# Seven block products in place of eight for the first layer's gate and up projections

## The chip, the cores and the metric

The kernel runs on one core of one Trainium2 chip. Its metric is the device time of one execution in microseconds (us); the comparison goes by the median of several runs. The engines are named as in the profile: PE (TensorE, matmul) with PEld (its weight loads), DVE (VectorE), ACT (ScalarE), POOL (GpSimd) and SP (SyncE, which issues the DMAs). Each engine takes its instructions in a fixed order.

## The reference

A backbone of two layers over 512 latent tokens and 256 context tokens, width 1024. Each layer has a mixing sub-layer and a SwiGLU sub-layer of inner width 2816. The context goes through the whole first layer; the second layer puts out the latent tokens alone.

```
def swiglu(h, w_gate, w_up, w_down):
    return (jax.nn.silu(h @ w_gate) * (h @ w_up)) @ w_down

x = x + g1 * (jnp.concatenate([y_a, y_b, y_c], axis=-1) @ w_out)
x = x + g2 * swiglu(modulate(x, norm2_g, sh2, sc2), w_gate, w_up, w_down)
...                          # the same for the context xc, while ctx_out
# modulate(x, g, shift, scale) = rms_norm(x, g) * (1 + scale) + shift
# mod = silu(c) @ w_mod[l] + b_mod[l]: shift, scale and gate of both sub-layers
```

## The kernel before

Features lie on the 128 partitions and tokens on the free axis, so `x` is eight tiles (k = 0 to 7) of 128 x 768. Every large product is done in fp32 accuracy by three matmuls of a shorter type: `split` writes a high half by an ACT copy and a low half by a DVE subtract, and hi·hi, hi·lo and lo·hi are summed in PSUM. `wload` loads a weight block of 128 x 1024 from DRAM (SP) into one of the `wraw` buffers and splits it (ACT L128, DVE L129). `dense` (L152) takes a block over nk steps of k, for each the three matmuls, for each 512 latent and then 256 context columns.

A SwiGLU sub-layer has 22 column blocks of gate and of up. In the first layer the blocks are worked through in three pieces, `FF_PIECES` = (0,8), (8,8), (16,6). Within a piece each block does gate, up, then `silu` on ACT, the product with up on DVE (L1177) and a split of the result into `gh`, `gl` (L108, L109). The first three blocks run as a wave (L402): all three advance with each k, while `norm2` delivers the normed k from DVE. At the end of a piece eight `dense` calls form the piece's share of the down projection, and `resid` adds each to `x` in SBUF (L1100).

The next layer's modulation rows (`mod_steps`) are computed beside this on DVE: a step loads a 512 KB block of `w_mod` and does one or two products with the sum over the free axis (L212, output to `junk` or in place). The steps wait in a list `fill`; each `dense` pops one (`FILL_FF` = 1). `lagged` runs w_out and the last piece of the down projection: it does the latent part of the last k before the context part, so that the norm that follows can begin.

The order of an engine's instructions comes from a list scheduler over the program, with its own costs; buffers come from pools, and SP issues all DMAs in one order, so a transfer that waits holds up those behind it.

Of the kernel before, what the change touches and what calls it, by code (L numbers as in the profile page):

```python
# [9 lines left out]
F32 = mybir.dt.float32  # L10
# [7 lines left out]
D = 1024  # L18
# [25 lines left out]
def tile_backbone(ctx: ExitStack, tc: tile.TileContext, A, out):  # L44
# [10 lines left out]
    wk = ctx.enter_context(tc.tile_pool(name="wk", bufs=7))  # L55
    tok = ctx.enter_context(tc.tile_pool(name="tok", bufs=1))
# [44 lines left out]
    def zct(name, dt=F32):  # L101
        return zc.tile([128, ZU], dt, tag="z", name=name)
# [97 lines left out]
    c_all = const.tile([128, 2, D], F32, name="c_all")  # L200
    junk = const.tile([128, D], F32, name="junk")

    def mod_steps(l, vs):
# [3 lines left out]
        def step(v, i):  # L207
# [3 lines left out]
            for t in range(nt):  # L211
                ve.scalar_tensor_tensor(  # L212
                    out=junk if t < nt - 1 else raw, in0=raw, scalar=1.0, in1=c_all[:, t, :], op0=ALU.mult, op1=ALU.mult,
                    accum_out=modT[:, v * 8 + i, t:t + 1])
# [228 lines left out]
    for l in range(2):  # L443
# [215 lines left out]
        def do_Crows():  # L659
            i64 = zct("i64")[:, 0:384].rearrange("p (c s) -> p c s", c=6)  # L660
            f64 = zct("f64")[:, 0:384].rearrange("p (c s) -> p c s", c=6)
            gp.memset(i64, 0.0)
# [434 lines left out]
        def resid(pss, k, row, gs):  # L1097
            for ps, g in zip(pss, gs):
                xs = xsl(k, g)
                ve.scalar_tensor_tensor(  # L1100
                    out=xs, in0=ps, scalar=modT[:, row * 8 + k, g[3]:g[3] + 1], in1=xs, op0=ALU.mult, op1=ALU.add)
# [39 lines left out]
        steps2 = []  # L1141
        preload(AF.Sqrt, tabled)
        lagged(lambda k: wload(A["w_out"][l, k]), KD,
               lambda g: (lambda k: yv(g, k, 0), lambda k: yv(g, k, 1), g[2]), 2, norm2, *TRAIL[2 * l])
        h_next = {}
        hp2 = [hpart(h2, g) for g in groups]
        W_g, W_u = A["w_gate"][l], A["w_up"][l]
        fill_rate[0] = FILL_FF
        if not last:
            fill.extend(mod_steps(0, (5,)) + mod_steps(1, range(6)))  # L1150
        for pi, (f0, nf) in enumerate(FF_PIECES):
# [97 lines left out]
def layout(inputs):  # L1249
# [18 lines left out]
    def ksplit(w, nk):  # L1268
# [34 lines left out]
```

## Time and profile before

| | before |
|---|---|
| median of 3 runs | 1716.52 us |
| lowest, highest | 1714.64, 1721.14 us |
| profiled execution | 1715.26 us |
| its span, granted clock | 1713.5 us, 0.988 |
| PE busy | 1654.2 us (97%), 10784 matmuls |
| DVE busy | 940.7 us (55%), 1697 instructions |
| DMA | 184.11 MB, mean 107 GB/s |

The span is what the profiler saw between the first and the last instruction; the execution's own time is a little longer. Busy shares are means over stages with different limits: the first layer's SwiGLU sub-layer runs from about 449 us to 1012 us, the second layer's ends the program. A timeline row gives start, duration, engine, line, operation and tiles, and in brackets the idle time ahead of it and what ended that. Durations of rows that follow each other overlap a little, so the difference of two starts is the pace.

### The profile page before, as it was taken

How to read it: one execution, taken by the hardware profiler on the slowest of the kernel's cores; microseconds unless marked ns; L12 is line 12 of the kernel's file. 1: busy time of each engine (PE TensorE's matmuls, PEld its weight loads, DVE VectorE, ACT ScalarE, POOL GpSimd, SP SyncE). 2: the span in 40 equal slices, each digit the busy share in tenths (PEclk: the TensorE clock that was granted, in tenths of full speed). 3: DMA queues.
4: the chain of work that ended last, by engine and by line, in shares of the span. 5: the costliest groups of instructions: out<-in, count | busy, mean ns of one | idle time of the engine just before them, and what ended most of it. 6: DMA issues, size and time to landing. Idle time of an engine off the chain costs nothing.

```text
span 1713.5 us, 26246 instructions
## 1 busy us (share of the span) xinstructions
PE 1654.2 (97%) x10784; PEld 1413.0 (82%) x10784; DVE 940.7 (55%) x1697; ACT 609.2 (36%) x1123; POOL 154.9 (9%) x157
## 2 busy tenths in 40 slices
PE   7998999999999999999999999989989999999998
PEld 5886777778888888888888889767869988888888
DVE  4599788654665654434443365765585633333335
ACT  5455344643432211221122344534554522222235
POOL 0001112133100000000000120013043000000000
PEclk9999999999999999999999999989999999999999
DMA  8741323122153334333332234111113322222222
GB/s 301 247 157 56 119 82 104 49 84 75 65 160 123 123 127 134 125 129 126 123 123 90 75 108 125 61 50 46 62 62 124 107 97 99 98 99 93 92 83 96
DMA packets 57143, 184.11 MB, mean 107 GB/s; under 512 B 6720, under 2 KB 8384, under 8 KB 56896
## 3 DMA queue, kind: packets, MB, share of 16 engines
q1 hardware_dynamic: 57024, 182.45, 32.5%
q8 instruction: 84, 1.38, 0.3%
q14 instruction: 35, 0.29, 0.0%
HBM read 175.08 MB, written 7.34 MB: 106 GB/s over the span
## 4 chain that ended last, share of the span: by engine, by line
PE 79%; DVE 10%; issue 3%; ACT 3%; DMA 2%; POOL 1%; SPq 0%; DVEq 0%; ACTq 0%; POOLq 0%
PE dps L152 63%; PE wps L402 5%; PE vps L647 3%; DMA wmod<-in_w_mod 1%; DVE wlo L129 1%; PE bops L542 1%; PE ptps L584 1%; PE bsps L542 1%; DVE nm L569 1%; PE nps L896 1%; DVE junk L212 1%; DVE rM L715 1%; DVE rF L706 1%; ACT pu L882 1%; ACT prob L572 1%
## 5 line engine op out<-in xcount | busy, mean ns | idle before, releaser
L128 ACT ACTIVATE whi<-wraw 128x1024 fp32r<-128x1024 f32 (+2 forms) x224 | 226.6, 1013 | 716.1 <-PE dps L152 450.1
L129 DVE TENSOR_TENSOR wlo<-wraw,whi 128x1024 fp32r<-128x1024 f32 (+2 forms) x224 | 264.8, 1183 | 164.1 <-ACT whi L128 160.6
L152 PE MATMUL dps<-h2ll,whi 128*128 128x512 f32 (+1 forms) x664 | 259.4, 392 | 0.0
L152 PE MATMUL dps<-h2lh,wlo 128*128 128x512 f32 (+1 forms) x664 | 258.9, 392 | 0.0
L152 PE MATMUL dps<-h2lh,whi 128*128 128x512 f32 (+1 forms) x664 | 257.9, 390 | 0.0
L152 PE MATMUL dps<-gh,wlo 128*128 128x512 f32 (+1 forms) x576 | 175.2, 340 | 0.0
L152 PE MATMUL dps<-gl,whi 128*128 128x512 f32 (+1 forms) x576 | 175.0, 340 | 0.0
L152 PE MATMUL dps<-gh,whi 128*128 128x512 f32 (+1 forms) x576 | 174.7, 340 | 0.0
L212 DVE SCALAR_TENSOR_TENSOR wmod<-wmod,c_all 128x1024 f32<-128x1024 f32 x80 | 98.9, 1236 | 101.1 <-DMA wmod<-in_w_mod 100.3
L152 PEld LDWEIGHTS dps<-h2lh,wlo 128*128 128x128 f32 x664 | 124.3, 188 | 28.4
L152 PEld LDWEIGHTS dps<-h2lh,whi 128*128 128x128 f32 x664 | 124.3, 188 | 28.2
L152 PEld LDWEIGHTS dps<-h2ll,whi 128*128 128x128 f32 x664 | 124.3, 188 | 26.9
L1100 DVE SCALAR_TENSOR_TENSOR x<-dps,modT,x 128x512 f32<-128x512 f32 (+1 forms) x112 | 65.3, 596 | 137.8 <-PE dps L152 137.5
L152 PE MATMUL dps<-lh,whi 128*128 128x512 f32 x336 | 136.8, 408 | 0.3 <-DVE ck L783 0.3
L152 PE MATMUL dps<-ll,whi 128*128 128x512 f32 x336 | 135.5, 403 | 1.2 <-DVE ll L109 1.2
L152 PE MATMUL dps<-lh,wlo 128*128 128x512 f32 x336 | 134.5, 400 | 0.0
L152 PEld LDWEIGHTS dps<-gl,whi 128*128 128x128 f32 x576 | 99.3, 188 | 13.3 <-DVE gl L109 0.2
L152 PEld LDWEIGHTS dps<-gh,wlo 128*128 128x128 f32 x576 | 99.3, 188 | 13.1
L152 PEld LDWEIGHTS dps<-gh,whi 128*128 128x128 f32 x576 | 99.1, 188 | 13.2
L212 DVE SCALAR_TENSOR_TENSOR junk<-wmod,c_all 128x1024 f32<-128x1024 f32 x48 | 58.8, 1225 | 78.4 <-DMA wmod<-in_w_mod 78.3
L1177 DVE TENSOR_TENSOR silu<-silu,dps 128x512 f32<-128x512 f32 (+1 forms) x64 | 37.3, 588 | 107.7 <-PE dps L152 107.7
L152 PE MATMUL dps<-h2cl,whi 128*128 128x256 f32 x328 | 92.8, 283 | 0.0
(320 smaller groups left out, 3108.7 us busy)
## 6 DMA issues: line engine op xcount, KB each, us to landing
wmod<-in_w_mod SPq DMA_DIRECT2D x80, 512.0 KB, 3.6
wraw<-in_w_up SPq DMA_DIRECT2D x42, 512.0 KB, 3.2
wraw<-in_w_gate SPq DMA_DIRECT2D x40, 512.0 KB, 3.2
wraw<-in_win_blk SPq DMA_DIRECT2D x34, 512.0 KB, 3.7
wraw<-in_w_down SPq DMA_DIRECT2D x32, 512.0 KB, 3.2
wraw<-in_w_out SPq DMA_DIRECT2D x19, 512.0 KB, 3.3
wraw<-in_w_down SPq DMA_DIRECT2D x21, 384.0 KB, 3.0
wraw<-in_win_cv SPq DMA_DIRECT2D x16, 408.0 KB, 3.2
```

The costliest lines, as they stand in the source:

```text
L128: ac.activation(out=hi[:, 0:n], in_=raw[:, 0:n], func=AF.Copy)
L129: ve.tensor_tensor(out=lo[:, 0:n], in0=raw[:, 0:n], in1=hi[:, 0:n].bitcast(F32), op=ALU.subtract)
L152: m = te.matmul(out=ps[:, 0:T], lhsT=wt[:, c], rhs=(flo if wh else fhi)(k), start=(k == 0 and wi == 0), stop=(k == nk - 1 and wi == 2),)
L212: ve.scalar_tensor_tensor(out=junk if t < nt - 1 else raw, in0=raw, scalar=1.0, in1=c_all[:, t, :], op0=ALU.mult, op1=ALU.mult, accum_out= ...
L402: m = te.matmul(out=ps[:, 0:T], lhsT=wt[:, cs_], rhs=(flo if wh else fhi)(k), start=(k == 0 and wi == 0), stop=(k == KD - 1 and wi == 2))
L542: m = te.matmul(*args, **kw)
L569: ve.tensor_reduce(out=nm, in_=sps[:, 0:n], axis=AX.X, op=ALU.max, negate=True)
L572: ac.activation(out=pt[:, 0:n], in_=sps[:, 0:n], func=AF.Exp, bias=nm, accum_out=sm_)
L584: te.transpose(out=tps[:, i * 128:(i + 1) * 128], in_=pt[:, i * 128:(i + 1) * 128], identity=ident)
L647: te.matmul(out=vps[i][:, 0:408], lhsT=tokslice(nm, k, i), rhs=wt[:, cs], start=(k == 0 and wi == 0), stop=(k == KD - 1 and wi == 2))
L1100: ve.scalar_tensor_tensor(out=xs, in0=ps, scalar=modT[:, row * 8 + k, g[3]:g[3] + 1], in1=xs, op0=ALU.mult, op1=ALU.add)
L1177: ve.tensor_tensor(out=s, in0=s, in1=pui, op=ALU.mult)
```

## The change

Only the first layer's SwiGLU sub-layer is rebuilt (`ffn_seven`), and what has to make room for it.

- Two column blocks are a pair and the tokens two halves of 384. The eight k are four even-odd couples j. So gate (or up) of a pair is a 2 x 2 by 2 x 2 block product, done with seven products P1 to P7 instead of eight. A `Unit` is the gate or the up of one pair, 22 in all. Each product is 4 j x 3 matmuls of 384 columns (L1260).
- The weight operands are sums of blocks: `s1`, `s2`, and a difference written over half of the second block (DVE L1239 to L1241), then `s4` (L1251); all are split. The activation operands T1 to T4 (L1185 to L1190) are made once, after the norm, by `operands`; B11, B21 and B22 are plain halves.
- The seven results meet in three PSUM tiles X, Y, Z. `snap` copies a partial sum out (ACT), `put` adds the other part (DVE L1285), multiplies with gate (L1289) and splits.
- `pin` fixes the order of the products on PE: P6 P5 P7 of a unit, P1 P2 of the next unit, then P4 P3 of the first.
- Six pieces of 2, 4, 4, 4, 4 and 4 column blocks (`FF0_PIECES`). `x` no longer stays in SBUF: for each k of a piece's down stage it is loaded from DRAM into `xs` (L1426), gets the residual (L1106) and is stored (L1428); the last piece loads it into tiles again.
- The pools: `wraw` 3 to 4 buffers, from which `junk` is now taken too; `wk` 7 to 9; small tiles moved into others.
- The eight steps of modulation row 5 of layer 0 move from the SwiGLU sub-layer to the mixing sub-layer, ahead of w_out. Layer 1's 48 steps stay in `fill`.

```
 FF_PIECES = [(0, 8), (8, 8), (16, 6)]
+FF0_PIECES = [(0, 2)] + [(f, 4) for f in range(2, 22, 4)]
+HN = 384
...
-    wraw = ctx.enter_context(tc.tile_pool(name="wraw", bufs=3))
+    wraw = ctx.enter_context(tc.tile_pool(name="wraw", bufs=4))
...
+        def operands(j):
+            e, o = hf[2 * j], hf[2 * j + 1]
+            n1, n2 = slice(0, HN), slice(HN, 2 * HN)
...
+                if ops[0] == "T1":
+                    ve.tensor_tensor(out=t[:, n1], in0=e[:, n2], in1=e[:, n1], op=ALU.subtract)
+                    ve.tensor_tensor(out=t[:, n2], in0=o[:, n2], in1=t[:, n1], op=ALU.subtract)
...
+                split(hi, lo, t[:, 0:2 * HN])
...
+            def sums(self):
+                a, b = self.a, self.b
+                self.s1, self.s2 = wkt("s1"), wkt("s2")
+                ve.tensor_tensor(out=self.s1, in0=b[:, 0:512], in1=b[:, 512:1024], op=ALU.add)
+                ve.tensor_tensor(out=self.s2, in0=self.s1, in1=a[:, 0:512], op=ALU.subtract)
+                ve.tensor_tensor(out=b[:, 0:512], in0=a[:, 0:512], in1=b[:, 0:512], op=ALU.subtract)
...
+            def put(self, q, d, ps):
+                g = self.spot(q)
+                if d is not None:
+                    ve.tensor_tensor(out=d if self.up else g, in0=d, in1=ps[:, 0:HN], op=ALU.add)
+                if not self.up:
+                    ac.activation(out=g, in_=ps[:, 0:HN] if d is None else g, func=AF.Silu)
+                    return
+                ve.tensor_tensor(out=g, in0=g, in1=ps[:, 0:HN] if d is None else d, op=ALU.mult)
+                th, tl = [t[q // 2][:, (q % 2) * HN:(q % 2) * HN + HN] for t in tiles(self.pr)]
+                split(th, tl, g)
...
+                        u.stage2()      # P6, P5, P7
+                        feed(1)
...
+                            nxt.stage1()    # P1, P2 of the next unit
+                        u.stage3()      # P4, P3
+                        if nxt is not None and i < nf - 1:
+                            nxt.fin1()
...
+                    for k in range(KD):
+                        xt = zat("xs")
+                        sp.dma_start(out=xt, in_=xd[k])
+                        resid(dense(dload(k), nf, [gpart(g) for g in whole], mm if k % 2 == 0 else mx), k, 5, whole, xt)
+                        sp.dma_start(out=xd[k], in_=xt)
...
+        if not last:
+            fill.extend(mod_steps(0, (5,)))
...
-            fill.extend(mod_steps(0, (5,)) + mod_steps(1, range(6)))
+            fill.extend(mod_steps(1, range(6)))
```

How this stands on DVE is shown at three places. A row has the line, the operation, output and inputs with buffer numbers, the shape, and the waits: PE and Activation are engines, DMAHW a DMA. The first place is the opening, just behind the second norm of the first layer. Before, the context part of the norm is written (`hn`, then its low half `h2cl` or `h2ll`):

```order
L286 SCALAR_TENSOR_TENSOR hn_4715<-x0_4136,a2_231,rb_4697 128x256 [waits Activation_49]
L286 SCALAR_TENSOR_TENSOR hn_4741<-x1_4137,a2_231,rb_4697 128x256
L286 SCALAR_TENSOR_TENSOR hn_4827<-x4_4140,a2_231,rb_4620 128x512
L288 SCALAR_TENSOR_TENSOR h2cl_4687<-hn_4715,modT_227,h2ch_4686 128x256 [waits Activation_49]
L288 SCALAR_TENSOR_TENSOR h2cl_4687<-hn_4741,modT_227,h2ch_4686 128x256 [waits Activation_49]
L286 SCALAR_TENSOR_TENSOR hn_4773<-x2_4138,a2_231,rb_4697 128x256 [waits DVE_49]
```

After, behind all of the norm (`hf`), the operands follow (T1 and T2 in one tile `t`, T3 and T4 in the next):

```order
L1185 TENSOR_TENSOR t_4934<-hf_4671 128x384
L1189 TENSOR_TENSOR t_4939<-hf_4672,hf_4671 128x384
L1186 TENSOR_TENSOR t_4934<-hf_4672,t_4934 128x384 [waits DVE_49]
L114 TENSOR_TENSOR ocl_4791<-hf_4678,och_4790 128x384
L1190 TENSOR_TENSOR t_4939<-hf_4672,t_4934 128x384 [waits DVE_49]
L114 TENSOR_TENSOR wlo_5053<-wraw_4804,whi_5052 128x1024 [waits Activation_49]
L114 TENSOR_TENSOR oll_4670<-t_4934,olh_4669 128x768 [waits Activation_49]
L114 TENSOR_TENSOR ol_4943<-t_4939,oh_4942 128x768 [waits Activation_49]
```

Sums of operands and two low halves of 768 now stand between the norm and the products P6 and P5 of a j; the list repeats for each j.

The second place is the down stage of the first piece. Before, for each k (24 matmul pairs of `dps` on PE) one low half, one step of modulation and one residual:

```order
L129 TENSOR_TENSOR wlo_6122<-wraw_6119,whi_6121 128x1024 [waits DMAHW4_49,Activation_49]
L212 SCALAR_TENSOR_TENSOR junk_104,modT_228<-wmod_6299,c_all_103 128x1024 [waits DMAHW1_49]
L212 SCALAR_TENSOR_TENSOR wmod_6299,modT_228<-wmod_6299,c_all_103 128x1024 [waits DVE_49]
L1100 SCALAR_TENSOR_TENSOR x3_4139<-dps_6001,modT_227,x3_4139 128x512 [waits PE_49]
L1100 SCALAR_TENSOR_TENSOR x3_4139<-dps_6002,modT_227,x3_4139 128x256 [waits PE_49]
L129 TENSOR_TENSOR wlo_6184<-wraw_6181,whi_6183 128x1024 [waits DMAHW6_49,Activation_49]
```

After, with 12 matmuls for a k, and one low half (512 wide) for two k:

```order
L1106 SCALAR_TENSOR_TENSOR xs_5279<-dps_5282,modT_226,xs_5279 128x256 [waits PE_49]
L216 SCALAR_TENSOR_TENSOR junk_5297,modT_227<-wmod_5295,c_all_103 128x1024 [waits DMAHW6_49,DVE_49]
L216 SCALAR_TENSOR_TENSOR wmod_5295,modT_227<-wmod_5295,c_all_103 128x1024 [waits DVE_49]
L134 TENSOR_TENSOR wlo_5308<-wraw_5305,whi_5307 128x512 [waits DMAHW2_49,Activation_49]
L216 SCALAR_TENSOR_TENSOR junk_5327,modT_227<-wmod_5325,c_all_103 128x1024 [waits DMAHW3_49,DVE_49]
L216 SCALAR_TENSOR_TENSOR wmod_5325,modT_227<-wmod_5325,c_all_103 128x1024 [waits DVE_49]
L1106 SCALAR_TENSOR_TENSOR xs_5303<-dps_5311,modT_226,xs_5303 128x512 [waits DMAHW4_49,DMAHW0_49,PE_49]
L1106 SCALAR_TENSOR_TENSOR xs_5303<-dps_5312,modT_226,xs_5303 128x256 [waits PE_49]
```

The low half for k = 4 and 5 (`wlo_5308`) stands behind the residual of k = 3, which waits for PE, and behind a modulation step; the residual now waits for a load of `xs` too.

The third place is within a pair, where gate hands over to up. Before, in a column block of the first piece (`silu` times up, low halves of weights and of `gl`):

```order
L1177 TENSOR_TENSOR silu_5142<-silu_5142,dps_5087 128x512 [waits PE_49,Activation_49]
L129 TENSOR_TENSOR wlo_5286<-wraw_5283,whi_5285 128x1024 [waits DMAHW2_49,PE_49,Activation_49]
L109 TENSOR_TENSOR gl_5141<-silu_5142,gh_5140 128x512 [waits Activation_49]
L1177 TENSOR_TENSOR silu_5147<-silu_5147,dps_5028 128x256
L212 SCALAR_TENSOR_TENSOR junk_104,modT_227<-wmod_5398,c_all_103 128x1024 [waits DMAHW5_49]
```

After, in the fifth piece, from the end of P2 of an up unit (`Y_8051`) to the low half that its P6 needs (`wlo_8125` from `s2_8120`); `Z_8006` is the gate unit's last product, P3:

```order
L1285 TENSOR_TENSOR sn_8064<-sn_8064,Y_8051 128x384 [waits PE_49,Activation_49]
L1289 TENSOR_TENSOR gate_7978<-gate_7978,sn_8064 128x384 [waits DVE_49]
L114 TENSOR_TENSOR gl_8115<-gate_7978,gh_8113 128x384 [waits Activation_49]
L1239 TENSOR_TENSOR s1_8119<-wraw_8043 128x512 [waits DMAHW0_49]
L1240 TENSOR_TENSOR s2_8120<-s1_8119,wraw_8042 128x512 [waits DVE_49]
L1241 TENSOR_TENSOR wraw_8043<-wraw_8042,wraw_8043 128x512
L114 TENSOR_TENSOR wlo_8125<-s1_8119,whi_8124 128x512 [waits Activation_49]
L1285 TENSOR_TENSOR gate_8004<-gate_8004,Z_8006 128x384 [waits PE_49]
L114 TENSOR_TENSOR wlo_8125<-s2_8120,whi_8124 128x512 [waits Activation_49]
```

Before, the low half of the next block's weights needs only its transfer, its high half and a free buffer; now the sums, a result that waits for P2 and one that waits for P3 stand ahead of it.

More of the change, by code (lines that the diff above doesn't have):

```diff
@@ L212, in step @@
                 ve.scalar_tensor_tensor(
-                    out=junk if t < nt - 1 else raw, in0=raw, scalar=1.0, in1=c_all[:, t, :], op0=ALU.mult, op1=ALU.mult,
+                    out=wraw.tile([128, D], F32, tag="w", name="junk") if t < nt - 1 else raw, in0=raw, scalar=1.0, in1=c_all[:, t, :], op0=ALU.mult, op1=ALU.mult,
                     accum_out=modT[:, v * 8 + i, t:t + 1])
@@ L1103, in tile_backbone, with lagged @@
         h2 = {}
-        def lagged(load, nk, part, row, done, tr, pos, eng=gp):
+        def lagged(load, nk, part, row, done, tr, pos, eng=gp, between=None):
             ga, gb = groups
@@ L1127, in lagged @@
                     done(ga, ssq[0])
+                if between is not None:
+                    between()
             done(gb, ssq[1])
@@ L1141, in tile_backbone, with norm2_seven, step @@
         steps2 = []
+        O, hf = {}, []
+        def norm2_seven(g, ssq):
+            s, o, T, m = g
+            n = 10 if m == 0 else 5
+            th = hyp.tile([128, n, HN], F32R, tag=s + "h", name="o" + s + "h")
+            tl = hyp.tile([128, n, HN], F32R, tag=s + "l", name="o" + s + "l")
+            O[s] = (th, tl)
+            if m == 0:
+                hf.extend(zct("hf") for _ in range(KD))
+            bc = ssq.finish(s)
+            def step(k):
+                v = hf[k][:, 512 * m:512 * m + T]
+                ve.scalar_tensor_tensor(
+                    out=v, in0=xsl(k, g), scalar=a2s[l][:, k, m:m + 1], in1=bc, op0=ALU.mult, op1=ALU.mult)
+                ac.activation(out=v, in_=v, func=AF.Identity, bias=modT[:, 3 * 8 + k, m:m + 1])
+                if m == 0:
+                    split(th[:, k, :], tl[:, k, :], hf[k][:, 0:HN])
+                    O["B%d1" % (1 + k % 2), k // 2] = (th[:, k, :], tl[:, k, :])
+                else:
+                    sp.dma_start(out=xd[k], in_=x[k][:, 0:768])
+            steps2.extend(lambda k=k: step(k) for k in range(KD))
@@ new lines, in feed, with ffn_seven, down, gpart @@
+        def feed(n):
+            for _ in range(min(n, len(fill))):
+                fill.pop(0)()
+        def ffn_seven():
+            nonlocal x
+            pairs = [p for f0, nf in FF0_PIECES for p in range(f0 // 2, (f0 + nf) // 2)]
+            units = []
+            for pr in pairs:
+                g = {}
+                units += [Unit(0, pr, g), Unit(1, pr, g)]
+            def down(pi):
+                f0, nf = FF0_PIECES[pi]
+                gh, gl = [], []
+                for pr in range(f0 // 2, (f0 + nf) // 2):
+                    gh += store[pr][0]
+                    gl += store[pr][1]
+                def gpart(g):
+                    o, T = (0, 512) if g[0] == "l" else (512, 256)
+                    return (lambda k: gh[k][:, o:o + T], lambda k: gl[k][:, o:o + T], T)
+                cache = {}
+                def dload(k):
+                    if k // 2 not in cache:
+                        cache.clear()
+                        cache[k // 2] = wload(A["w_dn0_%d" % pi][k // 2])
+                    c = (k % 2) * nf * 128
+                    return [t[:, c:c + nf * 128] for t in cache[k // 2]]
+                return nf, gpart, dload
+            u0, u1 = units[:2]
+            for u in (u0, u1):
+                u.w1()
+                u.banks1()
+            for u in (u0, u1):
+                u.sums()
+            some_steps(KD)
+            for j in range(4):
+                for u in (u0, u1):
+                    u.prod("P1", u.X, [j])
+                if j == 3:
+                    for u in (u0, u1):
+                        u.snap1()
+                for u in (u0, u1):
+                    u.prod("P2", u.Y, [j])
+            for u in (u0, u1):
+                u.w2()
+                u.Z = pst(mx, "Z")
+            for u in (u0, u1):
+                u.fin1()
+            for j in range(4):
+                operands(j)
+                for nm, at in (("P6", "X"), ("P5", "Z")):
+                    for u in (u0, u1):
+                        u.prod(nm, getattr(u, at), [j], start=(nm == "P5"))
+            for u in (u0, u1):
+                u.snap2()
+            for u in (u0, u1):
+                u.snap5()
+            for u in (u0, u1):
+                u.w3()
+                u.prod("P7", u.X, start=False)
+                u.fin22()
+            units[2].stage1()
+            u0.stage3()
+            u1.stage3()
+            nu = 2
+            for pi in range(len(FF0_PIECES)):
+                nf = FF0_PIECES[pi][1]
+                if pi:
+                    for i in range(nf):
+                        u = units[nu + i]
+                        u.stage2()
+                        feed(1)
+                        nxt = units[nu + i + 1] if nu + i + 1 < len(units) else None
+                        if nxt is not None:
+                            nxt.stage1()
+                        u.stage3()
+                        if nxt is not None and i < nf - 1:
+                            nxt.fin1()
+                    nu += nf
+                nf, gpart, dload = down(pi)
+                if pi < len(FF0_PIECES) - 1:
+                    for k in range(KD):
[3 more added lines that the diff above has]
+                        sp.dma_start(out=xd[k], in_=xt)
+                    pin[0] = last_pe[0]
+                    units[nu].fin1()
+                else:
+                    feed(len(fill))
+                    x = x_tiles()
+                    for k in range(KD):
+                        sp.dma_start(out=x[k][:, 0:768], in_=xd[k])
+                    def done(g, ssq):
+                        norm1_begin(1, h_next, x, groups.index(g), ssq)
+                    preload(AF.Sqrt)
+                    lagged(dload, nf, gpart, 5, done, *TRAIL[1], eng=gp)
```

157 lines of the change are left out of this document (143 added, 14 removed).

## The prediction

> **What bounds the kernel now.** I read the page's shares first, then the chain that ended last, then the stretch of the first layer's channel sub-layer (from 448.7 us) by engine.
>
> ```profile
> span 1713.5 us, 26246 instructions
> ...
> PE 1654.2 (97%) x10784; PEld 1413.0 (82%) x10784; DVE 940.7 (55%) x1697; ACT 609.2 (36%) x1123; POOL 154.9 (9%) x157
> ...
> PE 79%; DVE 10%; issue 3%; ACT 3%; DMA 2%; POOL 1%; SPq 0%; DVEq 0%; ACTq 0%; POOLq 0%
> ```
>
> ```profile
> 456.93 22.13 PE wps L402 x130
> 479.06 525.30 PE dps L152 x2970
> ```
>
> ```profile
> 1012.27 0.28 PE L152 MATMUL dps<-gh,wlo 128*128 128x256 f32 x1
> ```
>
> ```profile
> 330.00:393.00 63.00, 57.89 (x541) 46.40 (x540) 36.46 (x71) 33.28 (x77) 19.67 (x18) 0.97 0.22 74
> 448.70:479.00 30.30, 30.28 (x185) 26.53 (x184) 29.14 (x51) 17.06 (x29) 1.25 (x1) 1.00 0.34 112
> 479.00:1004.00 525.00, 525.00 (x2970) 456.36 (x2969) 237.58 (x358) 111.20 (x165) 11.06 (x12) 1.00 0.37 121
> 14.00:30.00 16.00, 12.43 (x100) 8.04 (x101) 9.63 (x25) 6.39 (x15) 0.00 (x0) 1.00 1.00 362
> ```
>
> The columns of the last view are the stretch, its length, busy PE, PEld, DVE, ACT and POOL, the granted clock, the DMA share and GB/s; the matmul at 1012.27 is the sub-layer's last, so from the norm it lasts 563.7 us. From 448.7 to 1004 PE has no hole at all: the sub-layer lasts as long as its matmuls, so matmuls removed there are time removed, and every hole that appears there is time added. DVE is busy 45% of the long stretch but 29.14 of 30.30 us in the opening, while the norm is applied. That opening is where the change puts more DVE work.
>
> **1. Fewer matmuls: -52.7 us.** Before, one weight block costs 8 x 3 pairs of a 512- and a 256-column matmul; there are 44 blocks.
>
> ```profile
> 698.42 1.06 ACT L128 ACTIVATE whi<-wraw 128x1024 fp32r<-128x1024 f32 x1 [4.78 <-PE dps L152]
> ...
> 706.90 1.06 ACT L128 ACTIVATE whi<-wraw 128x1024 fp32r<-128x1024 f32 x1 [6.94 <-issue]
> ```
>
> ```profile
> 700.53 0.28 PE L152 MATMUL dps<-h2ch,wlo 128*128 128x256 f32 x1
> 700.64 0.40 PE L152 MATMUL dps<-h2lh,whi 128*128 128x512 f32 x1
> 700.88 0.28 PE L152 MATMUL dps<-h2ch,whi 128*128 128x256 f32 x1
> ```
>
> ```profile
> 1399.78 0.39 PE L152 MATMUL dps<-h2lh,whi 128*128 128x512 f32 x1
> 1400.00 0.39 PE L152 MATMUL dps<-h2ll,whi 128*128 128x512 f32 x1
> ```
>
> ```profile
> 1313.63 0.28 PE L152 MATMUL dps<-yAh,whi 128*128 128x256 f32 x1
> 1313.75 0.28 PE L152 MATMUL dps<-yAl,whi 128*128 128x256 f32 x1
> ```
>
> One block takes 706.90 - 698.42 = 8.48 us, so 44 take 373.1. After, 22 units have 7 products x 4 x 3 = 84 matmuls of 384 columns, 1848 in all. No row has 384 columns. Start to start, 512 alone go at about 0.227 us (0.22 to 0.23 in such rows) and 256 alone at 0.12; halfway is 0.1734, and half of a mixed pair (8.48/48) is 0.1767. I take the first, since the new matmuls are of one size: 1848 x 0.1734 = 320.4, a saving of 52.7 (46.6 by the other). Each matmul has its own weight load before and after (x2970 against x2969), and the 256-column row shows that a load fits in 0.12 us. The down products keep their matmuls, so they cost the same when fed.
>
> **Prices on DVE.** The starts of rows that follow each other give the pace:
>
> ```profile
> 708.00 1.22 DVE L129 TENSOR_TENSOR wlo<-wraw,whi 128x1024 fp32r<-128x1024 f32 x1 [0.15 <-ACT whi L128]
> 709.14 0.68 DVE L109 TENSOR_TENSOR gl<-silu,gh 128x512 fp32r<-128x512 f32 x1
> 709.74 0.41 DVE L1177 TENSOR_TENSOR silu<-silu,dps 128x256 f32<-128x256 f32 x1
> 710.64 0.42 DVE L109 TENSOR_TENSOR gl<-silu,gh 128x256 fp32r<-128x256 f32 x1 [0.48 <-ACT gh L108]
> ```
>
> ```profile
> 448.74 2.08 DVE L286 SCALAR_TENSOR_TENSOR hn<-x,a,rb 128x512 f32<-128x512 f32 x3 [1.94 <-ACT rb L276]
> ...
> 452.45 0.95 DVE L129 TENSOR_TENSOR wlo<-wraw,whi 128x768 fp32r<-128x768 f32 x1
> 453.31 0.47 DVE L1100 SCALAR_TENSOR_TENSOR x<-dps,modT,x 128x256 f32<-128x256 f32 x1
> 453.71 0.84 DVE L288 SCALAR_TENSOR_TENSOR h2ll<-hn,modT,h2lh 128x512 fp32r<-128x512 f32 x1
> ```
>
> ```profile
> 599.20 1.14 DVE L1100 SCALAR_TENSOR_TENSOR x<-dps,modT,x 128x512 f32<-128x512 f32 x2
> 600.26 1.21 DVE L129 TENSOR_TENSOR wlo<-wraw,whi 128x1024 fp32r<-128x1024 f32 x1
> ...
> 605.09 1.22 DVE L212 SCALAR_TENSOR_TENSOR junk<-wmod,c_all 128x1024 f32<-128x1024 f32 x1 [3.62 <-DMA wmod<-in_w_mod]
> ...
> 606.35 1.22 DVE L212 SCALAR_TENSOR_TENSOR wmod<-wmod,c_all 128x1024 f32<-128x1024 f32 x1
> ```
>
> So 1024 wide 1.14, 768 0.86, 512 0.60 (0.67 with a scalar), 256 0.33 to 0.40, a residual pair 1.06, one modulation product 1.26 (1.22 and its read-out). For 384 wide I take 0.465, halfway between 0.60 and 0.33.
>
> **2. Opening: +26 us.** From the latent norm (448.74) to the last combined operand's low half, DVE now has, in its order: 8 x 0.67 + 8 x 0.40 for hf; 12 low halves of 384 (8 B11/B21, 4 B22), 16 operand sums and 4 rows of the first gate and up results, 32 x 0.465; 8 low halves of 768, 8 x 0.86; two of 1024, 2.3; five weight sums, two s4 and four low halves, 11 x 0.60; and 1.2 of residual and norm. That is 8.6 + 14.9 + 6.9 + 2.3 + 6.6 + 1.2 = 40.5. ACT must make each high half first; where the next low half is the next DVE row, nothing covers that (0.15 and 0.48 in the rows above), some 4 in all. So the fourth j is ready 44.5 after the norm. Behind it PE still has 12 + 24 + 24 + 48 = 108 matmuls, 18.7 us: end at 63.2. PE's work in that time is 192 x 0.1734 = 33.3 and about 3.7 of w_out; 26 us are holes, where it had none. Bounds: 18 if all rows no operand needs slip behind, 30 if each hand-off costs twice that.
>
> **3. First piece's down stage: +15 us.** With two column blocks a k is 12 matmuls, 2.1 us. DVE needs 1.06 for the residual, 0.3 for half a 512-wide low half, and 2.5 for the modulation step that each `dense` pops: 3.9. In its order the low half for the next two k stands behind the residual that waits for PE, and behind one or two modulation products; PE waits some 3.5 per two k. Four such waits, of 0.8 for the first and 3.5 to 4.0, make 11.8; the last result of the opening pair, with its modulation products in between, 3.4. Bounds: 7 (the rows overlap as they do at 599 to 606, where PE had no hole) and 23: weights, modulation rows and the residual's two ways are 13.7 MB in some 36 us, or 380 GB/s, against 362 at a share of 1.00, which can add 8.
>
> **4. Gate to up: +12 us.** After P2 of an up unit PE has only P4 and P3 of the gate unit, 24 x 0.1734 = 4.2, and 0.35 before it needs the low half of s2. DVE in that time must add and multiply (0.93), wait for ACT (0.6), make the low half (0.47), the three sums (1.8), the low half of s1 (0.6), then add Z, which ends with P3 (0.47), and the low half of s2 (0.6); with 0.3 for two releases it takes 5.8. The rest, 1.2, is a hole, at 10 pairs. From up to the next gate the low half stands ahead of the add and hides. Bounds 0.8 (the two rows behind the end of P3, less 0.35) and 2.0.
>
> **5. Later down stages: +5.** Four blocks give 4.2 us a k, and DVE needs 1.06 + 0.6 + up to 2.5. In the second piece SP issues later weights behind stores of x that wait for DVE: 3.9 there, 1 further on; 0 to 12. Nothing waited there before, because x stayed in place.
>
> **6. The clock: +10.**
>
> ```profile
> 250.23 2.05 PE L823 MATMUL sps<-cq,ck 64*128 64x128 f32 x16 [2.08 <-DVE rden L922]
> ```
>
> ```profile
> 248.00:256.00 8.00, 5.92 (x35) 4.30 (x34) 5.98 (x10) 1.85 (x4) 4.84 (x6) 0.64 0.32 94
> 256.00:264.00 8.00, 7.98 (x44) 6.83 (x43) 4.30 (x10) 3.42 (x12) 2.69 (x3) 0.72 0.10 39
> ```
>
> ```profile
> 344.00:346.00 2.00, 0.26 (x4) 0.11 (x4) 1.80 (x2) 0.28 (x1) 1.80 (x1) 0.97 0.00 0
> 346.00:348.00 2.00, 2.00 (x20) 2.00 (x22) 1.43 (x2) 0.00 (x0) 0.00 (x0) 0.50 0.05 14
> 348.00:350.00 2.00, 2.00 (x15) 1.59 (x12) 1.53 (x4) 0.00 (x0) 1.74 (x2) 0.68 0.71 244
> ```
>
> A hole of 2.08 us is followed by 0.64 and 0.72 over 16 us (5.1 us of work lost), one of 1.74 by 0.50 and 0.68 (1.6 lost). Smaller holes, 3.6 us in all from 14 to 30, left it at 1.00. The opening and the first piece are made of holes of 2 to 4 us: I take 3 for the work behind the opening, 3 behind the first piece, and 4 for its own 16.8 us of matmuls, part of which DVE hides. Bounds 0 and 25. The Trainium skill, "TensorE: Matmul & The Clock Gate", section "Part 1: The HAM clock gate", has half rate after an idle window of about 3.4 us and full rate after a busy one as long. By that page an event costs 1.7 us and only the longest holes count: about three events, +5, and a time of 1730. The rows disagree on both, since 1.74 us sufficed and the low clock outlasted 3.4 us once.
>
> **7. First layer's mixing: +4.** Sixteen modulation products (20 us of DVE) move there. From 330 to 393 DVE has 26.5 us free of 63, but its rows alternate with ACT and POOL, and a row of 1.26 in the way delays the next. Bounds 0 and 10. A fourth weight buffer for layer 1 hides behind a PE that is busy anyway: nothing.
>
> **Sum.** -52.7 + 26 + 15 + 12 + 5 + 10 + 4 = +19.3. The profiled execution took 1715.3 (span 1713.5), 1.3 under the median of 1716.5: 1734.6, so **1735**.
>
> **Rivals.**
> - *The hops between engines are hidden* (faster). Terms 2, 3 and 4 hold some 4, 2 and 8 us of one engine waiting for another's row. If the queues run ahead, these go, shorter holes keep the clock (10), and the mixing's 4 is covered in the same way: 1735 - 28 = 1707. It decides for faster when holes and clock together are under 44 us (52.7 - 8.6). For it: 0.15 at 708.00. Against: 0.48 at 710.64. With the opening also at its lower bound: 1699. Chance 0.20.
> - *The gains and holes cancel*: the opening at 18, hand-offs at 0.8, clock at 5: 1735 - 8 - 4 - 5 = 1718. Chance 0.25.
> - *Every hand-off drops the clock*: holes of 1.2 us grow to 1.7, and each of 10 pairs then loses 1.6 to 5.1; at 3, +30: 1765. Against: holes of that size from 14 to 30 at 1.00. Chance 0.10.
> - *The new matmuls don't go at their width* but at the mean weight load of these groups, 0.188: 1848 x 0.188 = 347, a saving of 26, 1762. Against: 0.12 at 256. Chance 0.05.
>
> ```profile
> L152 PEld LDWEIGHTS dps<-h2lh,wlo 128*128 128x128 f32 x664 | 124.3, 188 | 28.4
> ```
>
> - The forecast, 1726 to 1755 with some of its terms at a bound: 0.40.
>
> Half a per cent, 8.6 us, is about what the three runs before can tell from no change: 1707.9 to 1725.1. Faster 0.20, same 0.25, slower 0.55. The range, 1704 to 1762, leaves out half of the first rival, and of the slow ones the third and a few in a hundred.
>
> **What would show it.** PE rows of 384 columns 0.173 apart; holes of about 26 us in the 65 us behind the first layer's second norm, released by DVE; some 15 in the down stage behind it with granted clock below 0.8; 10 holes of about 1.2 us at L1260 released by the low half of s2; PE at 1.00 busy inside the pairs. If the stretch up to layer 1's first product is under 555 us instead of 563.7, the holes were over-counted; if holes stand at each pair with a clock under 0.9, term 6 was too small.

## The result, and the profile after

The changed kernel takes 1760.16 us (median of 4 runs, 1759.83 to 1763.4) against 1717.4 (1714.64 to 1721.14): a ratio of 1.0252, interval 1.0228 to 1.0275. It is slower, as forecast, but by 43 us, where the forecast had 18 to 19.

The page of the changed kernel: span, busy shares, the shares of the chain that ended last.

```profile
span 1758.1 us, 26467 instructions
...
PE 1631.4 (93%) x10520; PEld 1424.8 (81%) x10520; DVE 1109.1 (63%) x1983; ACT 693.4 (39%) x1273; POOL 164.4 (9%) x157
...
PE 67%; DVE 17%; DMA 6%; ACT 4%; issue 3%; POOL 2%; SPq 0%; DVEq 0%; ACTq 0%; POOLq 0%
```

PE is busy 23 us less and the span is 45 longer, so some 67 us of new holes stand in it. DVE's part of the chain went from 10 to 17%, that of DMA from 2 to 6%. Outside the first layer's SwiGLU sub-layer little moved: the norm is applied from 453.1 in place of 448.7, and from layer 1's first product (1057.1 and 1012.4) to the end both kernels take 701 us. The sub-layer takes 604.0 us in place of 563.7.

By stage, in the changed kernel (columns as in the prediction: stretch, length, PE, PEld, DVE, ACT, POOL, clock, DMA share, GB/s): the opening up to the first down product, the first piece's down stage, the second piece's products, its down stage, the third piece's products and down stage, the fifth's down stage.

```profile
453.10:523.70 70.60, 49.38 (x229) 45.30 (x227) 56.39 (x97) 37.97 (x68) 0.72 (x1) 0.78 0.18 62
523.70:560.70 37.00, 22.66 (x97) 18.84 (x98) 25.33 (x42) 3.88 (x6) 0.00 (x0) 0.77 0.69 230
560.70:628.30 67.60, 61.17 (x338) 59.57 (x337) 51.81 (x85) 27.10 (x45) 0.00 (x0) 0.97 0.42 135
628.30:670.90 42.60, 37.00 (x195) 31.55 (x194) 31.18 (x54) 5.69 (x7) 0.00 (x0) 0.92 0.76 252
670.90:732.90 62.00, 59.46 (x339) 58.18 (x338) 43.16 (x69) 27.22 (x45) 0.00 (x0) 1.00 0.45 144
732.90:767.20 34.30, 34.03 (x193) 29.38 (x192) 25.06 (x42) 5.82 (x7) 0.00 (x0) 1.00 0.82 269
929.70:963.50 33.80, 33.80 (x194) 29.46 (x193) 16.23 (x26) 4.95 (x7) 0.00 (x0) 1.00 0.60 199
```

| stage | by the prediction's terms | measured |
|---|---|---|
| opening: 37.0 of work, 26 + 3.4 of holes, 3 of clock | 69.4 | 70.6 |
| first down stage: 16.8, 11.8 of holes, 4 of clock | 32.6 | 37.0 |
| second piece's products: 58.3, two hand-offs, 3 of clock | 63.7 | 67.6 |
| its down stage: 33.5 + 3.9 | 37.4 | 42.6 |
| all behind 670.9: 229 of products, 134 of down stages, eight hand-offs, 1 | 373.5 | 386.2 |

By the table the miss is 27.4 us: 13.5 in the second to fourth rows, 12.7 in the last and 1.2 in the opening. (The middle column adds up to 576.6; the prediction's own terms give 579.0 for the same stretch, since the table's work is 2.4 us shorter.) In the last row PE's holes are 14.1 us in place of 10.6; about 5 more go where PE counts as busy but starts its rows later, mostly behind the hand-offs between gate and up; the rest, some 4, is small differences of pace.

PE's rows in and behind the first down stage, and a hand-off late in the kernel:

```profile
543.23 1.01 PE L157 MATMUL dps<-gh,whi 128*128 128x512 f32 x2 [8.65 <-ACT whi L133]
555.00 1.01 PE L157 MATMUL dps<-gh,whi 128*128 128x512 f32 x2 [5.24 <-ACT whi L133]
```

```profile
570.77 0.44 PE L1260 MATMUL X<-olh,whi 128*128 128x384 f32 x1 [3.63 <-ACT whi L113]
```

```profile
651.23 1.01 PE L157 MATMUL dps<-gh,whi 128*128 128x512 f32 x2 [4.58 <-ACT whi L133]
```

```profile
977.88 0.34 PE L1260 MATMUL Z<-och,wlo 128*128 128x384 f32 x1
978.50 0.44 PE L1260 MATMUL X<-olh,whi 128*128 128x384 f32 x1 [0.28 <-ACT whi L113]
978.78 0.34 PE L1260 MATMUL X<-oll,whi 128*128 128x384 f32 x1
980.11 0.44 PE L1260 MATMUL X<-olh,wlo 128*128 128x384 f32 x1 [0.99 <-DVE wlo L114]
980.38 0.33 PE L1260 MATMUL X<-oh,whi 128*128 128x384 f32 x1
```

From 977.88 to 980.38 four rows start in 2.50 us; at 0.174 each they would take 0.70. So a hand-off costs 1.8 us, of which 1.27 are shown as holes.

The longest hole behind 670.9, and the stretch behind it:

```profile
773.54 0.44 PE L1260 MATMUL X<-oh,whi 128*128 128x384 f32 x1 [1.97 <-ACT gate L1279]
```

```profile
773.50:776.00 2.50, 2.46 (x14) 2.46 (x15) 1.47 (x2) 0.89 (x2) 0.00 (x0) 1.00 0.91 249
```

What ended 8.65 and 5.24 is a high half, so one goes back from there to its transfer. DVE's rows and SP's issues around 540 and 551:

```profile
538.47 1.23 DVE L216 SCALAR_TENSOR_TENSOR junk<-wmod,c_all 128x1024 f32<-128x1024 f32 x1 [0.89 <-DMA wmod<-in_w_mod]
539.62 0.08 DVE L216 DVE_READ_ACCUMULATOR junk<-wmod,c_all 128x1 f32 x1
...
551.31 0.08 DVE L216 DVE_READ_ACCUMULATOR junk<-wmod,c_all 128x1 f32 x1
```

```profile
539.74 0.33 SPq L130 DMA_DIRECT2D wraw<-in_w_dn  x1
...
551.42 0.33 SPq L130 DMA_DIRECT2D wraw<-in_w_dn  x1
```

SP issues the next down weights 0.04 us after DVE has finished a `junk` row, and PE goes on 3.5 us later, when transfer and high half are done. What SP's issues waited for in this stage (523.7 to 560.7) says the same of the weights (L130): total us, times, longest. L1428 are the stores of x, L1426 its loads.

```profile
SPq L1428 <- DVE xs L1106: 8.8, 6, 1.9
SPq L130 <- DVE junk L216: 8.3, 3, 4.4
SPq L213 <- DVE junk L216: 4.1, 1, 4.1
SPq L1426 <- DMA xd<-xs: 4.0, 2, 2.2
```

The weights waited for a buffer: a modulation step with two products holds two of the four `wraw` buffers, `wmod` and `junk`, until DVE has come to it. The transfers of x wait too, for the residual and for buffers of `xs`, and stand ahead of weights in SP's order; the experiments have to tell the two apart.

### The profile page after: what moved, and what is told of

The parts are those of the page before. It is cut to its first block, busy times and chain, and to the rows that moved or that the text cites. A ratio compares the mean times of both kernels' runs of the same rounds, so it can differ in the third digit from the quotient of the medians.

```text
span 1758.1 us, 26467 instructions
## 1 busy us (share of the span) xinstructions
PE 1631.4 (93%) x10520; PEld 1424.8 (81%) x10520; DVE 1109.1 (63%) x1983; ACT 693.4 (39%) x1273; POOL 164.4 (9%) x157
## 4 chain that ended last, share of the span: by engine, by line
PE 67%; DVE 17%; DMA 6%; ACT 4%; issue 3%; POOL 2%; SPq 0%; DVEq 0%; ACTq 0%; POOLq 0%
PE dps L157 39%; PE X L1260 8%; DMA wmod<-in_w_mod 4%; PE wps L406 4%; PE Z L1260 3%; PE vps L652 3%; PE Y L1260 2%; DVE junk L216 1%; DVE wlo L134 1%; DVE wmod L216 1%; PE ptps L588 1%; PE bops L546 1%; PE bsps L546 1%; DVE wlo L114 1%; DVE nm L573 1%
## 5 line engine op out<-in xcount | busy, mean ns | idle before, releaser
L133 ACT ACTIVATE whi<-wraw 128x1024 fp32r<-128x1024 f32 (+3 forms) x178 | 179.3, 1008 | 470.1 <-PE dps L157 247.6
L134 DVE TENSOR_TENSOR wlo<-wraw,whi 128x1024 fp32r<-128x1024 f32 (+3 forms) x178 | 209.7, 1178 | 134.4 <-ACT whi L133 129.5
L157 PE MATMUL dps<-h2ll,whi 128*128 128x512 f32 (+1 forms) x336 | 128.0, 384 | 0.0
L157 PE MATMUL dps<-h2lh,whi 128*128 128x512 f32 (+1 forms) x336 | 128.0, 384 | 0.0
L157 PE MATMUL dps<-h2lh,wlo 128*128 128x512 f32 (+1 forms) x336 | 127.9, 384 | 0.0
L1106 DVE SCALAR_TENSOR_TENSOR x<-dps,modT,x 128x256 f32<-128x256 f32 (+1 forms) x80 | 47.0, 589 | 115.7 <-PE dps L157 115.3
L216 DVE SCALAR_TENSOR_TENSOR wmod<-wmod,c_all 128x1024 f32<-128x1024 f32 x80 | 101.3, 1267 | 27.4 <-DMA wmod<-in_w_mod 26.7
L1260 PE MATMUL X<-oh,whi 128*128 128x384 f32 x242 | 83.1, 343 | 6.7 <-ACT gate L1279 3.5
L114 DVE TENSOR_TENSOR wlo<-wraw,whi 128x1024 fp32r<-128x1024 f32 (+1 forms) x66 | 67.8, 1042 | 33.5 <-ACT whi L113 33.4
L157 PE MATMUL dps<-ch,whi 128*128 128x256 f32 x256 | 75.0, 293 | 11.4 <-DVE bv L525 7.5
L1260 PE MATMUL X<-ol,whi 128*128 128x384 f32 x242 | 82.5, 341 | 0.6 <-DVE ol L114 0.6
L1260 PE MATMUL X<-oh,wlo 128*128 128x384 f32 x242 | 82.4, 340 | 0.0
```

The source lines that it names most:

```text
L114: ve.tensor_tensor(out=lo, in0=src, in1=hi.bitcast(F32), op=ALU.subtract)
L133: ac.activation(out=hi[:, 0:n], in_=raw[:, 0:n], func=AF.Copy)
L134: ve.tensor_tensor(out=lo[:, 0:n], in0=raw[:, 0:n], in1=hi[:, 0:n].bitcast(F32), op=ALU.subtract)
L157: m = te.matmul(out=ps[:, 0:T], lhsT=wt[:, c], rhs=(flo if wh else fhi)(k), start=(k == 0 and wi == 0), stop=(k == nk - 1 and wi == 2),)
L216: ve.scalar_tensor_tensor(out=wraw.tile([128, D], F32, tag="w", name="junk") if t < nt - 1 else raw, in0=raw, scalar=1.0, in1=c_all[:, t, ...
L1106: ve.scalar_tensor_tensor(out=xs, in0=ps, scalar=modT[:, row * 8 + k, g[3]:g[3] + 1], in1=xs, op0=ALU.mult, op1=ALU.add)
```

## The experiments

Times are medians. The kernel before measured 1715.1, 1714.6 and 1716.7 us beside the three groups of runs (e1 to e4, e5 to e8, e9 to e12); ratios are to it. The changed kernel's 1760.16 comes from a group in which the kernel before measured 1717.4, so a difference to 1760.16 is 2 to 3 us smaller by the ratios in e1 to e8; a gain under 5 us is not shown by the times alone.

**e1, no modulation steps in the first down stage.**

```
                 nf, gpart, dload = down(pi)
+                fill_rate[0] = 0 if pi == 0 else FILL_FF
```

> The down stage of the first piece pops no modulation steps; the same 48 steps are done later. In the changed kernel this stage (520.6 to 571.2) loses 27 us: 21 of holes and 6 of low clock. Theory A (buffers: a modulation step holds two of the four weight buffers, wmod and junk, so the next down weights are issued only when DVE has done it, as at 539.62 and 539.74): 15 to 20 us of the 27 go, with 4 back in the second piece, whose down stage now gets the two-product steps: about 1746. Theory B (the transfers of x and weights fill the DMA engines): only 4.2 of 13.7 MB go, holes shrink by 5 to 8: about 1753. Theory C (the low clock is what costs): holes go but the stage stays at 0.83: about 1756.

1742.98 us, 1.0164 (1.0145 to 1.0183): 17 us less (15 by the ratios). Opening, first and second down stage of e1:

```profile
453.80:524.60 70.80, 49.39 (x228) 45.87 (x226) 55.27 (x94) 39.22 (x70) 0.73 (x1) 0.81 0.17 58
524.60:544.00 19.40, 19.35 (x100) 16.66 (x101) 11.50 (x19) 2.95 (x5) 0.00 (x0) 0.91 0.66 227
607.20:655.00 47.80, 37.14 (x193) 31.52 (x193) 34.08 (x56) 5.69 (x7) 0.00 (x0) 0.89 0.64 217
```

The first down stage falls from 37.0 to 19.4, with x streamed at 227 GB/s and no hole. The steps with two products now stand in the second, which grows from 42.6 to 47.8. That is theory A's size. B and C are out as the main cause in this stage: x still moves beside the weights, and the clock rose to 0.91 with the holes gone.

**e2, junk out of the weight pool.**

```
-    wk = ctx.enter_context(tc.tile_pool(name="wk", bufs=9))
+    wk = ctx.enter_context(tc.tile_pool(name="wk", bufs=8))
...
+    junk = const.tile([128, D], mybir.dt.bfloat16, name="junk")
...
-                    out=wraw.tile([128, D], F32, tag="w", name="junk") if t < nt - 1 else raw, ...
+                    out=junk if t < nt - 1 else raw, ...
```

> junk gets a tile of its own again, in a 2-byte type for room, and the wk pool has 8 buffers instead of 9; all else as changed. Theory A: the holes of 8.65 and 5.24 us in the first piece and 4.58 in the second, each of which ends one load after a junk row, go in large part: about 1747, with no hole over 5 us in the down stages. Theory B: same transfers, same time, 1760.

1747.67 us, 1.0197 (1.0174 to 1.0219): 12.5 less (9 by the ratios), in size what A said, though the profiled execution (1753) is the longest of its four runs and shows only half of it. Two down stages, and the hole that stays with the issue and the high half ahead of it:

```profile
523.10:555.20 32.10, 21.66 (x96) 17.75 (x97) 23.77 (x41) 3.88 (x6) 0.00 (x0) 0.79 0.65 223
624.00:666.40 42.40, 37.45 (x194) 31.91 (x193) 30.34 (x51) 5.78 (x8) 0.00 (x0) 0.92 0.72 250
```

```profile
542.73 1.01 PE L157 MATMUL dps<-gh,whi 128*128 128x512 f32 x2 [9.20 <-ACT whi L133]
```

```profile
535.47 0.32 SPq L1427 DMA_DIRECT2D xs<-xd  x1
535.84 0.63 SPq L130 DMA_DIRECT2D wraw<-in_w_dn  x1
```

```profile
542.05 0.63 ACT L133 ACTIVATE whi<-wraw 128x512 fp32r<-128x512 f32 x1 [16.76 <-DMA wraw<-in_w_dn]
```

The first is 5 us shorter, but one hole of 9.20 stays, against the expectation, and the second hardly changes. Ahead of this hole the weights waited for no junk row: they were issued 0.37 behind a load of x, and from issue to high half it took 6.2 us, where the 8.65 hole had 2.8. Junk's buffer is a part of the loss; what e1 takes away beyond that is the step itself: its own buffer, its transfer between those of x, its DVE rows.

**e3, Z's row behind the up unit's halves.**

```
                 self.prod("P3", self.Z, start=False)
+                if nxt is not None:
+                    nxt.sums()
+                    nxt.w2()
                 self.put(1, self.d2, self.Z)
```

> Within a pair, the sums and halves of the up unit's second weights are emitted ahead of the row that adds Z, the gate unit's last result. The hole in front of each up unit's P6 is 0.28 + 0.99 us now. If that row is what stands in the way, some 0.5 to 1.1 us go at 10 pairs: 1749 to 1755. If DVE's other rows or the weight buffers on the path of the high half (the 0.28) set it, the holes stay: 1760.

1755.45 us, 1.0238 (1.0208 to 1.0268). The same hand-off as 978.50 above, in e3:

```profile
972.55 0.44 PE L1260 MATMUL X<-olh,whi 128*128 128x384 f32 x1 [0.28 <-ACT whi L113]
973.69 0.45 PE L1260 MATMUL X<-olh,wlo 128*128 128x384 f32 x1 [0.53 <-DVE wlo L114]
```

0.46 us go at nine of the 10 pairs and 0.55 at the first, and the time falls by 4.7, just short of the range; by the ratios it is 2.4 and the intervals overlap, so it is the trace that shows the gain. The row that adds Z was a third of the hole. What holds the rest, a high half of 0.28 and a low half of 0.53, no run tried.

**e4, x not stored.** The line `sp.dma_start(out=xd[k], in_=xt)` behind the residual is left out.

> Left out: the 40 stores of x after a piece's residual (15.7 MB), so that the residual of all pieces but the last is lost; loads of x stay. Theory B: the down stages of the first four pieces, at 230 to 238 GB/s and a share of 0.7, lose a third of x's traffic, and SP no longer waits for DVE's residual: 15 to 25 us go, 1735 to 1745. Theory A: the weights still wait for buffers: 1752 to 1760.

1755.81 us, 1.0239 (1.0218 to 1.026): 4 us, 2 by the ratios, with overlapping intervals. The first two down stages again:

```profile
523.00:559.80 36.80, 23.33 (x97) 19.41 (x98) 26.42 (x44) 3.88 (x6) 0.00 (x0) 0.72 0.56 170
627.60:669.80 42.20, 37.00 (x193) 31.63 (x193) 31.75 (x55) 5.80 (x7) 0.00 (x0) 0.92 0.62 212
```

With 170 in place of 230 GB/s the first stage is as long as before. Theory B falls as the main cause. The loads of x were in every version of the changed kernel; no run leaves them out.

**e5 and e6, the operand sums.** In e5 `t` is a plain half (`e` for T1 and T2, `o` for T3 and T4). In e6 the four `ve.tensor_tensor` of `operands` are `gp.tensor_tensor`.

> Left out: the sixteen sums that make the operands T1 to T4; plain halves are split in their place, so the products are of other data with the same shapes. DVE has 16 x 0.465 = 7.4 us less in the opening. If the opening is DVE's row sum (the prediction's second step: 40.5 of DVE and 4 of hand-offs), the 70.6 us from the norm to the first down product fall by 6 to 8: 1752 to 1755. If it is ACT's high halves, the low clock or the wait for the weights, they fall by less than 3.

> The same sixteen sums are made by POOL, which is idle in the opening. If POOL makes a 384-wide sum in about the time of DVE, the opening falls by 5 to 8 us as without the sums: 1753. If POOL is twice as slow or holds DVE back, no change or a loss: 1760 to 1766.

e5: 1751.86 us, 1.0226 (1.0194 to 1.0258). The opening of e5:

```profile
453.80:514.00 60.20, 44.63 (x228) 42.03 (x228) 48.10 (x81) 37.22 (x69) 0.73 (x1) 0.83 0.21 72
```

60.2 in place of 70.6 us, 10 for 7.4 us of rows, more than the 6 to 8 expected. So the opening is set by DVE's rows and what hangs on them: leaving out a sum also takes away ACT's wait for it. e6: 1760.35 us, 1.027 (1.0246 to 1.0294), no gain. POOL needs 1.07 to 1.77 us, as means of the four lines, for a sum that costs DVE 0.47.

**e7, the thin piece last** (`FF0_PIECES` ends with (20, 2) in place of starting with (0, 2), and the first piece's loop runs over its second pair).

> The piece of two column blocks comes last instead of first: five pieces of four, then one of two. The first down stage then has 4.2 us of matmuls a k instead of 2.1. If the thin stage is what lets DVE, the modulation steps and the weight buffers fall behind, its 20.3 us of lost time go down to the 8.8 that the first piece of four had, and the last thin stage, with no modulation steps in it, loses under 5: 1745 to 1752. If the modulation steps with two products do it wherever they stand, the first down stage loses some 15 as well: 1755 to 1762.

1752.75 us, 1.0223 (1.0197 to 1.0248). First and last down stage of e7:

```profile
551.30:597.80 46.50, 37.23 (x194) 31.66 (x194) 34.27 (x57) 5.69 (x7) 0.00 (x0) 0.93 0.68 223
1024.50:1049.20 24.70, 21.96 (x112) 18.92 (x112) 17.64 (x27) 13.92 (x26) 12.33 (x11) 0.85 0.57 183
```

Between the two: the first stage loses 13 us with four blocks as well (33.5 is its work), so in the changed kernel the two-product steps cost in either stage, though less than in a thin one. The last, thin stage takes 24.7 for 16.8 of down products, more than the loss of 5 that was expected.

**e8, PE kept busy.**

```
+                        if pi == 0 and k % 2 == 1:
+                            wps = pst(md, "warm")
+                            for i in range(16):
+                                m = te.matmul(out=wps[:, 0:HN], lhsT=O["B22", 0][0][:, 0:128], rhs=O["B22", 0][0], ...)
```

> Added: 16 idle matmuls of 384 columns (2.8 us at full rate) behind each second k of the first piece's down stage, into a bank that nothing reads, so that PE is busy in part of the holes. Theory C (low clock): the granted clock of that stage, 0.77, rises to 0.95 or more, and of its 6 us and the 2.6 behind it 4 to 7 go: 1754. If DVE and the buffers set the pace of the stage and the low clock only fills waiting time: clock up, time the same or up to 5 longer.

1762.87 us, 1.0285 (1.0256 to 1.0314).

```profile
527.30:567.70 40.40, 34.11 (x161) 30.40 (x162) 28.74 (x48) 3.88 (x6) 0.00 (x0) 0.83 0.65 220
567.70:630.40 62.70, 59.69 (x337) 58.11 (x336) 48.39 (x79) 27.27 (x45) 0.00 (x0) 1.00 0.41 140
```

Neither theory quite: the clock rose only from 0.77 to 0.83, the stage grew by 3.4, the stage behind it shrank by 4.9 at a clock of 1.00, and the total did not gain. As far as a rise of 0.06 can tell, the low clock in the first down stage is no separate price there.

**e9 and e10, parts of the change in the kernel before.** e9 uses five pieces of four blocks and one of two for its first layer. e10 has `fill.extend(mod_steps(0, (5,)))` ahead of w_out in place of behind it.

> The kernel before, with only the piece sizes of its first layer changed: five pieces of four column blocks and one of two, x resident, junk on its own tile, three weight buffers. A k of a down stage is then 4.2 us of matmuls while DVE needs 1.06 + 0.6 + up to 2.5 and one load of 256 KB. If short k's with two-product modulation steps starve PE by themselves, the first such stages lose 5 to 9 us each as in the changed kernel: 1728 to 1735. If it takes junk in the weight pool and x's transfers on SP, the loss is under 5 us in all: 1715 to 1720.

> The kernel before, with only the eight steps of the first layer's row 5 moved from the SwiGLU sub-layer to ahead of w_out. The prediction's seventh step: +4 in the mixing stage, which is 448.7 to the norm now and 453.1 in the changed kernel. If that step alone did it, the norm comes 3 to 5 us later and the total is 1718 to 1721. If the delay comes from the other pools and the norm's new order, the norm comes within 1 us of 448.7 and the time is that of before.

e9: 1722.33 us, 1.0033 (1.0021 to 1.0045).

```profile
490.00:540.00 50.00, 50.00 (x285) 43.32 (x284) 32.63 (x57) 9.27 (x17) 0.00 (x0) 1.00 0.39 120
700.00:800.00 100.00, 100.00 (x570) 87.01 (x569) 51.01 (x83) 20.13 (x32) 0.00 (x0) 1.00 0.47 147
1000.00:1020.00 20.00, 15.95 (x85) 13.66 (x84) 17.75 (x29) 12.54 (x27) 12.43 (x12) 0.83 0.66 217
```

That is 2 us above the second range and 6 below the first. k's of 4.2 us with the same modulation steps leave no hole in PE when x is resident, junk has its tile and DVE makes no operands; what it costs comes from the thin last piece. A k of 2.1 us with two-product steps and x resident was not run. e10: 1716.9 us, 0.9994 (0.9979 to 1.001), no change. Its norm comes 3.2 us later, but so does all of that execution from the first layer's input products on; from the first attention score to the norm's ACT row it takes 357.2 us, against 357.8 before and 364.1 in the changed kernel. So the moved steps alone don't lengthen the stretch.

**e11 and e12, the repairs together.** e11 is e1, e2 and e3 in one; e12 also has no step popped by `dense` in the second down stage, but one for two k.

```
-                fill_rate[0] = 0 if pi == 0 else FILL_FF
+                fill_rate[0] = 0 if pi < 2 else FILL_FF
...
+                        if pi == 1 and k % 2 == 1:
+                            feed(1)
```

> e1, e2 and e3 together: no modulation steps in the first down stage, junk out of the weight pool, Z's row late. If the three gains (17, 12 and 5 us) are separate losses, 1726; since the first two share the first piece's stage, I expect 1731 to 1737. Seven products with both repairs stay slower than before as long as the opening loses 33 us.

> As e11, and in the second piece's down stage one modulation step for two k in place of one for each; all 48 steps are still done before the last piece. If the two-product steps are what loses time there (10.7 us of holes in e1), 5 to 9 us go against e11: 1724 to 1730. If weights or x set the pace there, as e11.

e11: 1731.26 us, 1.0088 (1.006 to 1.0115). e12: 1727.89 us, 1.0062 (1.0044 to 1.0081). Opening, first, second and third down stage of e12:

```profile
452.30:523.10 70.80, 49.45 (x228) 45.93 (x226) 55.28 (x94) 39.22 (x70) 0.73 (x1) 0.81 0.17 58
523.10:541.70 18.60, 18.57 (x96) 16.06 (x97) 11.65 (x20) 2.99 (x5) 0.00 (x0) 0.91 0.65 225
605.80:639.70 33.90, 33.85 (x194) 29.42 (x193) 26.31 (x44) 6.09 (x8) 0.00 (x0) 1.00 0.80 277
700.90:742.20 41.30, 35.83 (x193) 30.48 (x192) 30.80 (x52) 5.84 (x9) 0.00 (x0) 0.96 0.74 258
```

The second down stage is at its work with x streamed at 277 GB/s; the hole has gone to the third, 34.3 in the changed kernel, which now gets two-product steps. Both times lie in their expected ranges; the 3.4 us between e11 and e12 are not clear of noise, but the second stage falls from 39.3 to 33.9. Together some 32 of the 43 us come back. The opening, 70 us for 37 of work, is untouched. The experiments point to no version that beats the kernel before.

## Why the prediction was right or wrong

The direction was right; the size was too small by 25 us.

- **Products.** Twelve matmuls of 384 columns take 2.08 to 2.09 us on the changed kernel's chain, 0.174 each, as forecast. But PE's busy time in the sub-layer fell by only 21.5 us (563.7 to 542.2), since rows in and behind the holes take longer.
- **Opening.** 70.6 against 69.4, and e5 confirms that DVE's rows set it: the last operand's low half ends 48.0 behind the norm, where the forecast had 44.5. How the time divides was forecast less well: 21.2 of holes in place of 29.4, and 12.4 of longer rows in place of 3, so the close fit is in part luck. Half of the holes, 10.6, end with ACT's high half of an operand (`olh`, `oh`), which had waited 1 to 3 us for one of DVE's sums.
- **First and later down stages: the steps that failed.** Terms 3 and 5 priced DVE's order and the transfers, and the sentence on the fourth weight buffer gave the pool no cost at all. In its place the runs showed that a two-product step holds two of four buffers till DVE reaches it, and SP's next weights stand behind. Losses beyond the work, holes and clock together, were 20 us in the first down stage (forecast 16), 9 in the second (4) and about 9 in the products between them (5). e1 and e11 show that the steps do it, and e2 that junk's buffer is a part. e4 shows that x's stores are not the main cause, and e9 that k's of 4.2 us with these steps cost nothing with x resident and junk on its own tile. The bound of term 3 that priced the transfers at 380 GB/s was not met: the stage ran at 230, a share of 0.69.
- **Hand-offs: term 4 was mis-sized.** The hole is 1.27 at nine of 10 pairs, against 1.2. But the term counted the hole alone, and the rows behind it start late: the whole costs 1.8, some 6 us more over 10 pairs. The cause was put down half right: e3 shows that Z's row is 0.46 of it, and the first 0.28 ends with ACT's high half.
- **The clock.** The mechanism is there, 0.77 to 0.78 in the opening and the first down stage. As a term of its own it was not needed in these: e8 changed what PE did in the holes and won nothing. Hand-off holes of 0.99 us left the clock at 1.00, and so did the hole of 1.97 at 773.54, so the rival in which every one drops it falls. (Its evidence was weaker than it said: no hole of PE from 14 to 30 in the kernel before is over 0.97.) The Trainium skill, "TensorE: Matmul & The Clock Gate", section "Part 1: The HAM clock gate", has the clock fall after about 3.4 us of idling. That the holes of 0.99 and 1.97 us do nothing agrees with it; the clock of 0.50 behind a hole of 1.74 us, in the prediction's rows, does not. So the length of a hole alone doesn't settle it here.
- **By kind of loss** the miss looks different. Over the sub-layer the holes are 61.8 us, against 58 from terms 2 to 5. What was far too small is PE's time in longer rows, 34 us beyond the work at full pace, against 10 in term 6. In the opening and the first down stage such rows stand where PE would have waited anyway, by e5 and e8; how much of the 34 is a price of its own stays open beyond the 5 us at the late hand-offs.
- **Mixing.** The norm came 4.4 later, against 4, but not by the moved steps: e10 has them without the delay. So the number was luck. What does it, the changed pools or another part of the change, was not tried.
- **Rivals.** Hops were not hidden. The matmuls do go at their width.

What stays open: how the loss of the two-product steps divides between their buffer, their transfer and their DVE rows beside x (e2 took away only junk's buffer and left a hole of 9.20).

## What to carry to other kernels

A pool that two kinds of work share is a queue: ask how long each holds its buffer, and whose turn on which engine gives it back. A saving on the engine that is full is worth what the engine that feeds it can keep up with; here DVE's share went from 55 to 63%, and its row sums at one place, the opening, took back over half of the 52.7 us that the products save. Work that fills idle time in long stages (8.5 us a k) is no filler in short ones (2.1 us).

## What the runs showed of the hardware that I had not expected

While POOL makes the sums in e6, DVE's rows in the same time get longer. DVE in e6, ahead of POOL's first sums and beside them:

```profile
469.05 0.48 DVE L1164 SCALAR_TENSOR_TENSOR hf<-x,a,rb 128x256 f32<-128x256 f32 x1
469.45 0.69 DVE L1240 TENSOR_TENSOR s<-s,wraw 128x512 f32<-128x512 f32 x1
...
470.66 6.66 DVE L1164 SCALAR_TENSOR_TENSOR hf<-x,a,rb 128x256 f32<-128x256 f32 x7
477.24 2.90 DVE L114 TENSOR_TENSOR wlo<-s,whi 128x512 fp32r<-128x512 f32 x2
```

POOL's first sum starts at 470.16. Seven rows take 0.95 each where one took 0.40, and two of 512 take 1.45 each in place of 0.60: what DVE no longer does, it loses in longer rows.
